# First four column tiles side by side, gate projections moved around the gated linear unit, one more step in the cross attention

## The chip, the cores and the metric

The kernel runs on one core of one Trainium2 chip. The metric is the device time of one execution in microseconds (us), less is better. TensorE does the matmuls, ScalarE (ACT in the profile) the activations and copies, VectorE (DVE) the elementwise arithmetic, GpSimd (POOL) a few helpers; SyncE (SP) issues the DMAs. Each engine takes its instructions in program order and waits on semaphores for the others.

## What is computed

One block of a transformer over 512 rows of 1024 columns, in single precision. The parts that the change touches:

```python
h = rmsnorm(x, g_mix_pre[l])
proj = h @ w_in[l]
a_out = pool_mixer(proj[..., OFF_POOL:OFF_ATT], pool_w[l], pool_scale[l])
b_out = dilated_attention(proj[..., OFF_ATT:OFF_SSM], rel_bias)
c_out = s5_mixer(proj[..., OFF_SSM:OFF_SGU], ...)      # ends in g * sigmoid(g @ w_glu + b_glu), g = gelu(y)
d_out = sgu_mixer(proj[..., OFF_SGU:OFF_GATE], ...)
gates = sigmoid(proj[..., OFF_GATE:].reshape(B, S, N_BRANCH, D_MODEL) + gate_b[l])
merged = sum over the four branches of gates[:, :, i] * (branches[i] @ w_up[l, i])
x = x + rmsnorm(merged @ w_out[l], g_mix_post[l])
x = x + rmsnorm(cross_attn(rmsnorm(x, g_x_pre[l]), rmsnorm(mem, g_mem[l]), w_cq[l], w_ckv[l], w_co[l]), g_x_post[l])
x = x + rmsnorm(square(relu(rmsnorm(x, g_ff_pre[l]) @ w_ff1[l])) @ w_ff2[l], g_ff_post[l])
```

The cross attention has four heads of 128 columns over 256 memory rows.

## The kernel before

Every large product is made of three matmuls: each operand is split into a high part (rounded to the matmul's format, a copy on ScalarE, L140) and a low part (the rest, a subtraction on VectorE, L144, L146, L208 or L310), and `mm3` (L237 to L239) adds high x high, low x high and high x low in one PSUM bank. There are eight banks, used in turn. Names with h and l at the end are the two parts: xh and xl of the input, wh and wl of a weight chunk, hh and hl of the normalized rows, bh and bl of a branch, cph and cpl of the transposed attention weights.

Weights come as chunks of 512 KB in one fixed order (`chunk_order`); `fetch` lets SP load the next one, `issue` splits it (the copy wh on ScalarE, L140, the subtraction wl on VectorE, L208), `chunk` hands the next one out and demands that the order fits. A chunk "P" in that order is split early and kept for later.

Everything that follows a matmul is a Python generator: each `yield` is one step. `later(g)` puts it in a list (`fore`, or `back` for long-running ones), and `tick()`, called between groups of 12 matmuls, lets every generator in the lists take one step and feeds the weight queue. So the place of an instruction in its engine's order is set by how many yields stand ahead of it, and by how many ticks the main program makes.

The start (L275 to L318, `first_pair`, `first`): the eight tiles xk of the input and the first two weight chunks arrive in pieces in turn; f0 and f1, the first two of six column tiles f, are done together, six matmuls for each k of eight, then f2 to f5 one after another, 24 matmuls each. `start()` squares the tiles xk on ScalarE (L646), adds them on VectorE (acc, L648 and L651), sums them over the partitions on TensorE (ssq, L329), and builds from them the row scale R (rb on TensorE, L341). It is a generator in `back`.

The gated linear unit (glu): y (L562) of the last of four groups goes through a gelu on ScalarE (gy); the loop `while len(gy) < 4: tick()` waits for the fourth; then the four gy are split (bh and bl), two ticks are made, and 48 matmuls glu follow. All the time a generator of the dilated attention runs in `back`: score matmuls L (L874, L876), exponentials Pm (L894), transposes PT (L900), outputs oA and oB (L923), spread by rA and rB (L997, L998). `gates` behind the glu makes, for each of four pairs of columns, two gate projections pj (24 matmuls each, then a Tanh gt on ScalarE, L803) and the products up.

The cross attention (`cross`, L1243 on): for each head and each half of the rows a generator does q split (cq), scores cL, row maxima, exponentials, their normalization (cP on VectorE, L1268), transposes (cT on TensorE, L1273), the split of these (cph, cpl), the product co with the values, and the split of that (bh and bl). Behind it the output projection nat takes pairs of chunks.

Of the kernel before, what the change touches and what calls it, by code (L numbers as in the profile page):

```python
# [52 lines left out]
def chunk_order():  # L53
# [5 lines left out]
    def gates(b):  # L59
        r = []  # L60
        for cp in range(4):
            r += [("L", "w_in", OFF_GATE + b * D + 128 * c) for c in (2 * cp, 2 * cp + 1)]
            r += [("U", "w_up", b, cp)]
        return r
# [9 lines left out]
    o += [("U", "w_glu", 0, cp) for cp in range(2)]  # L74
    o += gates(2)
# [10 lines left out]
    for c in range(4):  # L86
        o += [("L", "w_cq", 128 * c)]
        if c in (1, 3):
            o += [early.pop(0)]
# [15 lines left out]
def body(ctx: ExitStack, tc: tile.TileContext, xT, xn, memT, wch, vec, rows, cst, biasT, poolw, wsT, bst, cbd, out):  # L105
# [33 lines left out]
    def acopy(o, i, scale=1.0):  # L139
        act.activation(out=o, in_=i, func=AF.Copy, scale=scale)  # L140
# [18 lines left out]
    def later(g):  # L159
        fore.append(g)  # L160
# [22 lines left out]
    def fetch(parts=1):  # L183
        raw = wraw.tile([P, 1024], F32, name="wr", tag="wr")
        for i in range(parts):
            c = slice(1024 * i // parts, 1024 * (i + 1) // parts)
            sp.dma_start(out=raw[:, c], in_=wch[at[0]][:, c])
        raws.append(raw)
        at[0] += 1
# [89 lines left out]
    pair = [wraw.tile([P, 1024], F32, name="wr", tag="wr") for _ in range(2)]  # L279
    sp.dma_start(out=vt, in_=vec)  # L280
    for n, c in enumerate(PIECES):
        for j in range(2):
            sp.dma_start(out=pair[j][:, c], in_=wch[j][:, c])
            sp.dma_start(out=xk[2 * n + j], in_=xT[:, 2 * n + j])
    for k in (6, 7):
        sp.dma_start(out=xk[k], in_=xT[:, k])
    at[0] = 2
    fetch()
# [15 lines left out]
    pair_hl = [[whl.tile([P, 1024], F32R, name=n, tag="w") for n in ("wh", "wl")] for _ in range(2)]  # L304
    for n, c in enumerate(PIECES):
        for j in range(2):
            hi, lo = pair_hl[j]
            acopy(hi[:, c], pair[j][:, c])
            xsplit(2 * n + j)
            dve.tensor_sub(out=lo[:, c], in0=pair[j][:, c], in1=f32(hi[:, c]))  # L310
    for k in (6, 7):
        xsplit(k)
    at[1] = at[2] = 2
# [308 lines left out]
    def first_pair():  # L622

        bs = [bank(f"f{j}") for j in range(2)]
        for k in range(8):
            for j in range(2):
                hi, lo = (t[:, P * k:P * k + P] for t in pair_hl[j])
                mm3(bs[j], hi, lo, xh[k], xl[k], k == 0, k == 7)
        return bs
# [12 lines left out]
    def start():  # L642
        acc = [G("acc"), G("acc")]
        for k in range(8):
            sq = acc[k] if k < 2 else G("sq")
            act.activation(out=sq, in_=xk[k], func=AF.Square)  # L646
            if k > 1:
                dve.tensor_add(out=acc[k % 2], in0=acc[k % 2], in1=sq)  # L648
            if k == 3:
                issue()  # L650
        dve.tensor_add(out=acc[0], in0=acc[0], in1=acc[1])  # L651
        next(params)
        yield
        yield
# [47 lines left out]
    fb[0], fb[1] = first_pair()  # L702
    next(st_gen)
    sp.dma_start(out=pw, in_=poolw)
    back.append(st_gen)
    for i in range(2, 6):
        fb[i] = first(i)
# [88 lines left out]
    def gates(bi, br, last=None):  # L796
        bh, bl = br
        for cp in range(4):
            gt = {}

            def gate(c, b):
                gt[c] = G("gt")
                act.activation(out=gt[c], in_=b, func=AF.Tanh, scale=0.5, bias=gbh[:, 8 * bi + c:8 * bi + c + 1])  # L803
                yield
# [14 lines left out]
            for c in (2 * cp, 2 * cp + 1):  # L819
                later(gate(c, proj(("L", "w_in", OFF_GATE + bi * D + 128 * c), kth(hh), kth(hl))))  # L820
# [213 lines left out]

    while len(gy) < 4:
        tick()
# [23 lines left out]
    gates(2, ca)  # L1060
# [183 lines left out]
    def cross(c, s, b):  # L1244
# [33 lines left out]
        lo_of(pl, ph, tb)  # L1278
        yield
# [220 lines left out]
```

## Time and profile before

| what | value |
|---|---|
| median of 3 runs | 1148.78 us (1148.76 to 1148.9) |
| the profiled execution | 1150.06 us |
| its span | 1148.3 us |
| TensorE (PE) busy | 1133.5 us, 99% |
| VectorE (DVE) busy | 728.5 us, 63% |
| ScalarE (ACT) busy | 502.4 us, 44% |
| GpSimd (POOL) busy | 119.0 us, 10% |
| chain that ended last: PE, DVE, ACT | 93%, 3%, 1% |
| granted TensorE clock, mean | 0.995 |

The span runs from the first to the last instruction of the profiled execution; the time of an execution holds a little more (1.76 us here). A busy share is the share of the span in which an engine had work; TensorE's clock is given as a share of its full speed. The chain that ended last follows the work back from the last instruction to whatever released it.

### The profile page before, as it was taken

The page shows a single profiled execution, that of the slowest core. Times are in us where ns is not written, and L with a number is a line of the kernel's source. Part 1 is how long each engine was busy: PE and PEld are TensorE (multiplying, and loading weights), DVE is VectorE, ACT ScalarE, POOL GpSimd, SP SyncE. Part 2 cuts the span into 40 slices and gives each one's busy share as a digit, 9 for nine tenths or more (in the row PEclk, how much of TensorE's full clock was granted, in tenths as well). Part 3 has the DMA queues.
Part 4 walks back from the last instruction along what each step waited for, and adds up shares of the span by engine and source line. Part 5 has one row for each costly group of instructions (what it writes and reads, how often), then busy time and mean ns, then how long its engine had stood idle before and what let it go on. Part 6 is the DMA issues. An engine that isn't in the chain of part 4 may idle for free.

```text
span 1148.3 us, 15062 instructions
## 1 busy us (share of the span) xinstructions
PE 1133.5 (99%) x5720; PEld 943.6 (82%) x5720; DVE 728.5 (63%) x1185; ACT 502.4 (44%) x962; POOL 119.0 (10%) x200
## 2 busy tenths in 40 slices
PE   8999999999999999989999999999999999999997
PEld 6888887888987787767888888999988888888886
DVE  6798999997688677554355737777433334445343
ACT  7354444433446665564243436554332234344341
POOL 6960200000000000200100005003000000000001
PEclk9999999999999999989999999999999999999999
DMA  7523235323233222212243462710222332332221
GB/s 240 173 86 111 94 114 151 113 82 112 78 97 112 78 77 92 74 37 92 86 138 107 159 208 78 226 46 20 74 92 92 100 102 92 95 108 96 88 74 74
DMA packets 40025, 119.69 MB, mean 104 GB/s; under 512 B 5136, under 2 KB 7184, under 8 KB 39952
## 3 DMA queue, kind: packets, MB, share of 16 engines
q1 hardware_dynamic: 39952, 118.73, 32.2%
q8 instruction: 45, 0.74, 0.3%
q14 instruction: 28, 0.23, 0.1%
HBM read 113.47 MB, written 2.10 MB: 101 GB/s over the span
## 4 chain that ended last, share of the span: by engine, by line
PE 93%; DVE 3%; ACT 1%; issue 1%; SPq 1%; DMA 1%; POOL 0%; DVEq 0%; POOLq 0%; ACTq 0%
PE pj L237 16%; PE pj L239 15%; PE pj L238 15%; PE nat L237 10%; PE nat L238 10%; PE nat L239 10%; PE up L237 2%; PE up L238 2%; PE up L239 2%; PE PT L900 1%; PE f L239 1%; PE f L237 1%; PE f L238 1%; PE oA L923 1%; PE L L874 1%
## 5 line engine op out<-in xcount | busy, mean ns | idle before, releaser
L208 DVE TENSOR_TENSOR wl<-wr,wh 128x1024 fp32r<-128x1024 f32 x183 | 223.8, 1227 | 106.7 <-ACT wh L140 106.0
L140 ACT ACTIVATE wh<-wr 128x1024 fp32r<-128x1024 f32 (+1 forms) x189 | 194.4, 1032 | 65.3 <-PE pj L238 36.2
L237 PE MATMUL pj<-hh,wh 128*128 128x512 f32 x496 | 198.4, 400 | 0.0
L239 PE MATMUL pj<-hh,wl 128*128 128x512 f32 x496 | 193.7, 390 | 0.0
L238 PE MATMUL pj<-hl,wh 128*128 128x512 f32 x496 | 193.4, 390 | 0.0
L237 PEld LDWEIGHTS pj<-hh,wh 128*128 128x128 f32 x496 | 93.2, 188 | 21.7 <-issue 1.2
L239 PEld LDWEIGHTS pj<-hh,wl 128*128 128x128 f32 x496 | 93.1, 188 | 20.1
L238 PEld LDWEIGHTS pj<-hl,wh 128*128 128x128 f32 x496 | 93.3, 188 | 18.8 <-issue 0.5
L237 PE MATMUL nat<-wh,fh 128*128 128x512 f32 x256 | 99.6, 389 | 0.0
L238 PE MATMUL nat<-wl,fh 128*128 128x512 f32 x256 | 99.6, 389 | 0.0
L239 PE MATMUL nat<-wh,fl 128*128 128x512 f32 x256 | 99.6, 389 | 0.0
L144 DVE TENSOR_TENSOR fl<-f,fh 128x512 fp32r<-128x512 f32 x60 | 40.5, 691 | 73.3 <-PE nat L238 71.2
L237 PE MATMUL pj<-h3h,wh 128*128 128x512 f32 x216 | 84.0, 389 | 0.0
L238 PE MATMUL pj<-h3l,wh 128*128 128x512 f32 x216 | 84.0, 389 | 0.0
L239 PE MATMUL pj<-h3h,wl 128*128 128x512 f32 x216 | 84.0, 389 | 0.0
L1342 DVE TENSOR_TENSOR f<-fr,pj 128x512 f32<-128x512 f32 x32 | 22.0, 688 | 97.5 <-ACT fr L1340 97.5
L140 ACT ACTIVATE t<-tS,Ms 128x32 f32<-128x32 f32 (+1 forms) x64 | 25.3, 395 | 122.2 <-DVE tS L517 113.6
L140 ACT ACTIVATE fh<-f 128x512 fp32r<-128x512 f32 x60 | 37.0, 630 | 89.0 <-PE nat L238 85.7
L1340 ACT ACTIVATE fr<-pj 128x512 f32<-128x512 f32 x32 | 19.2, 599 | 116.8 <-PE pj L239 116.8
L237 PEld LDWEIGHTS nat<-wh,fh 128*128 128x128 f32 x256 | 48.1, 188 | 10.0
L238 PEld LDWEIGHTS nat<-wl,fh 128*128 128x128 f32 x256 | 48.1, 188 | 9.9
L239 PEld LDWEIGHTS nat<-wh,fl 128*128 128x128 f32 x256 | 48.1, 188 | 9.9
(327 smaller groups left out, 2312.5 us busy)
## 6 DMA issues: line engine op xcount, KB each, us to landing
wr<-in_wch SPq DMA_DIRECT2D x188, 512.0 KB, 3.5
row<-in_rows SPq DMA_DIRECT2D x13, 256.0 KB, 6.2
xk<-in_xT SPq DMA_DIRECT2D x8, 256.0 KB, 5.3
U<-uh SPq DMA_DIRECT2D x32, 64.0 KB, 2.0
bias<-in_biasT SPq DMA_DIRECT2D x8, 256.0 KB, 3.9
x<-in_xn SPq DMA_DIRECT2D x8, 256.0 KB, 5.2
out_dram<-x SPq DMA_DIRECT2D x8, 256.0 KB, 2.0
braw<-in_bst SPq DMA_DIRECT2D x16, 96.0 KB, 3.6
```

The source lines that it names most:

```text
L140: act.activation(out=o, in_=i, func=AF.Copy, scale=scale)
L144: dve.tensor_sub(out=lo, in0=src, in1=f32(hi))
L208: dve.tensor_sub(out=lo[:, c], in0=raw[:, c], in1=f32(hi[:, c]))
L237: pe.matmul(out=o, lhsT=lh, rhs=rh, start=start, stop=False)
L238: pe.matmul(out=o, lhsT=lh, rhs=rl, start=False, stop=False)
L239: pe.matmul(out=o, lhsT=ll, rhs=rh, start=False, stop=stop)
L874: pe.matmul(out=L[:, lo:lo + 256], lhsT=q[0][a][e, s], rhs=k[0][b][e, ks], start=n == 0, stop=n == 2)
L900: pe.transpose(out=b[:, s:s + 128], in_=Pm[:, s:s + 128], identity=ident)
L923: pe.matmul(out=o_[O][e, s], lhsT=V[v][:, cs], rhs=o[h][:, 128 * n:128 * n + 128], start=n == 0 or n == 2 or (n == 1 and i == 0), stop=n % ...
L1340: act.activation(out=r, in_=b, func=AF.Relu)
L1342: dve.tensor_mul(out=t, in0=r, in1=b)
```

## The change

Four things, by place in the program:

- The start. Four weight chunks (in place of two) arrive in pieces, in turn with the tiles xk, and are split in pieces; `first_four` does f0 to f3 side by side, 12 matmuls for each k; only f4 and f5 go one after another. The generator `start()` runs up to its first yield ahead of these matmuls, and gets its next two steps from within them, behind k = 5 and behind k = 6; it has two yields less ahead of ssq.
- The glu. The two gate projections of the first column pair of the third branch (`gate_pair(2, 0)`) stand ahead of the loop that waits for the gelu, those of the second pair behind the glu matmuls, and `gates` takes them as given. The chunk order follows.
- One early chunk "P" stands behind the third w_cq chunk, not the fourth.
- `cross` has one more yield between the split cph, cpl and the product co.

```diff
@@ -71,8 +71,8 @@
     for hp in range(NPAIR):
         for g in range(3):
             o += [("L", "w_in", OFF_Q + 512 * g + 128 * hp), ("L", "w_in", OFF_K + 512 * g + 128 * hp)]
-    o += [("U", "w_glu", 0, cp) for cp in range(2)]
-    o += gates(2)
+    ahead = gates(2)
+    o += ahead[:2] + [("U", "w_glu", 0, cp) for cp in range(2)] + ahead[3:5] + [ahead[2]] + ahead[5:]
     o += gates(1)
     early = [("P", "w_ff1", 128 * c) for c in range(NPRE)]
     for h in range(2):
@@ -85,7 +85,7 @@
         o += [("R", "w_ckv", k, 512)]
     for c in range(4):
         o += [("L", "w_cq", 128 * c)]
-        if c in (1, 3):
+        if c in (1, 2):
             o += [early.pop(0)]
     o += [("R", "w_co", k, 512 * h) for k in range(2) for h in range(2)]
     o += [("L", "w_ff1", 128 * c) for c in range(NPRE, 32)]
@@ -276,16 +276,19 @@
     xl = [G("xl", F32R) for k in range(8)]
 
     PIECES = (slice(0, 256), slice(256, 512), slice(512, 1024))
-    pair = [wraw.tile([P, 1024], F32, name="wr", tag="wr") for _ in range(2)]
+    four = [[t[:, c] for c in PIECES] for t in (wraw.tile([P, 1024], F32, name="wr", tag="wr") for _ in range(3))]
+    g0, g1 = G("wr0"), G("wr1")
+    four.append([g0[:, 0:256], g0[:, 256:512], g1])
     sp.dma_start(out=vt, in_=vec)
     for n, c in enumerate(PIECES):
-        for j in range(2):
-            sp.dma_start(out=pair[j][:, c], in_=wch[j][:, c])
-            sp.dma_start(out=xk[2 * n + j], in_=xT[:, 2 * n + j])
-    for k in (6, 7):
-        sp.dma_start(out=xk[k], in_=xT[:, k])
-    at[0] = 2
-    fetch()
+        ks = (2 * n, 2 * n + 1) if n < 2 else (4, 5, 6, 7)
+        for j in range(4):
+            if j % 2 and j // 2 < len(ks):
+                sp.dma_start(out=xk[ks[j // 2]], in_=xT[:, ks[j // 2]])
+            sp.dma_start(out=four[j][n], in_=wch[j][:, c])
+        for k in ks[2:]:
+            sp.dma_start(out=xk[k], in_=xT[:, k])
+    at[0] = 4
     sp.dma_start(out=ct, in_=cst)
     dve.memset(ones, 1.0)
     dve.memset(mhalf, -0.5)
@@ -301,16 +304,18 @@
         acopy(xh[k], xk[k], gx(k))
         lo_of(xl[k], xh[k], xk[k], gx(k))
 
-    pair_hl = [[whl.tile([P, 1024], F32R, name=n, tag="w") for n in ("wh", "wl")] for _ in range(2)]
+    four_hl = [[whl.tile([P, 1024], F32R, name=n, tag="w") for n in ("wh", "wl")] for _ in range(4)]
     for n, c in enumerate(PIECES):
-        for j in range(2):
-            hi, lo = pair_hl[j]
-            acopy(hi[:, c], pair[j][:, c])
-            xsplit(2 * n + j)
-            dve.tensor_sub(out=lo[:, c], in0=pair[j][:, c], in1=f32(hi[:, c]))
-    for k in (6, 7):
-        xsplit(k)
-    at[1] = at[2] = 2
+        ks = (2 * n, 2 * n + 1) if n < 2 else (4, 5, 6, 7)
+        for j in range(4):
+            hi, lo = four_hl[j]
+            acopy(hi[:, c], four[j][n])
+            if j % 2 == 0 and j // 2 < len(ks):
+                xsplit(ks[j // 2])
+            dve.tensor_sub(out=lo[:, c], in0=four[j][n], in1=f32(hi[:, c]))
+        for k in ks[2:]:
+            xsplit(k)
+    at[1] = at[2] = 4
 
     def rstd(o, ss, n, scale):
 
@@ -619,13 +624,15 @@
         yield from split(pa[0][g], pa[1][g], o, vt[:, V_POOLS + g:V_POOLS + g + 1])
 
 
-    def first_pair():
-
-        bs = [bank(f"f{j}") for j in range(2)]
+    def first_four(beside):
+
+        bs = [bank(f"f{j}") for j in range(4)]
         for k in range(8):
-            for j in range(2):
-                hi, lo = (t[:, P * k:P * k + P] for t in pair_hl[j])
+            for j in range(4):
+                hi, lo = (t[:, P * k:P * k + P] for t in four_hl[j])
                 mm3(bs[j], hi, lo, xh[k], xl[k], k == 0, k == 7)
+            if k in (5, 6):
+                next(beside)
         return bs
 
     def first(i):
@@ -647,11 +654,10 @@
             if k > 1:
                 dve.tensor_add(out=acc[k % 2], in0=acc[k % 2], in1=sq)
             if k == 3:
+                fetch()
                 issue()
         dve.tensor_add(out=acc[0], in0=acc[0], in1=acc[1])
         next(params)
-        yield
-        yield
         yield
         sb = bank("ssq")
         sums(sb, acc[0], 4)
@@ -699,11 +705,11 @@
     next(params)
     st_gen = start()
     fb = [None] * 6
-    fb[0], fb[1] = first_pair()
     next(st_gen)
+    fb[:4] = first_four(st_gen)
     sp.dma_start(out=pw, in_=poolw)
     back.append(st_gen)
-    for i in range(2, 6):
+    for i in range(4, 6):
         fb[i] = first(i)
     dve.tensor_scalar(out=gbh, in0=vt[:, V_GATEB:V_GATEB + 32], scalar1=0.5, scalar2=None, op0=MUL)
     dve.tensor_scalar(out=bgh, in0=vt[:, V_BGLU:V_BGLU + 4], scalar1=0.5, scalar2=None, op0=MUL)
@@ -793,15 +799,22 @@
 
     merged = {}
 
-    def gates(bi, br, last=None):
+    def gate_pair(bi, cp):
+        gt = {}
+
+        def gate(c, b):
+            gt[c] = G("gt")
+            act.activation(out=gt[c], in_=b, func=AF.Tanh, scale=0.5, bias=gbh[:, 8 * bi + c:8 * bi + c + 1])
+            yield
+
+        for c in (2 * cp, 2 * cp + 1):
+            later(gate(c, proj(("L", "w_in", OFF_GATE + bi * D + 128 * c), kth(hh), kth(hl))))
+        return gt
+
+    def gates(bi, br, last=None, ahead=None):
         bh, bl = br
         for cp in range(4):
-            gt = {}
-
-            def gate(c, b):
-                gt[c] = G("gt")
-                act.activation(out=gt[c], in_=b, func=AF.Tanh, scale=0.5, bias=gbh[:, 8 * bi + c:8 * bi + c + 1])
-                yield
+            gt = ahead[cp] if ahead and cp < 2 else gate_pair(bi, cp)
 
             def up(c, b, gt):
                 if c not in merged:
@@ -816,8 +829,6 @@
                 if last:
                     yield from last(c)
 
-            for c in (2 * cp, 2 * cp + 1):
-                later(gate(c, proj(("L", "w_in", OFF_GATE + bi * D + 128 * c), kth(hh), kth(hl))))
             wh, wl = chunk("U", "w_up", bi, cp)
             for cc in range(2):
                 b = bank("up")
@@ -1032,6 +1043,7 @@
         back.append(run())
 
 
+    ahead = [gate_pair(2, 0)]
     while len(gy) < 4:
         tick()
     ga = branch()
@@ -1057,7 +1069,8 @@
                 mm3(b, wh[:, cc, k], wl[:, cc, k], ga[0][k], ga[1][k], k == 0, k == 3)
             tick()
             later(glu(2 * cp + cc, b))
-    gates(2, ca)
+    ahead.append(gate_pair(2, 1))
+    gates(2, ca, ahead=ahead)
     while back:
         tick()
     WB[0] = NBIG // 2
@@ -1276,6 +1289,7 @@
         ph, pl = G("cph", F32R), G("cpl", F32R)
         acopy(ph, tb)
         lo_of(pl, ph, tb)
+        yield
         yield
         o = bank("co")
         for m in range(2):
```

Where it moves instructions, in three places. `[waits ...]` names the engines, or DMA queues, on which an instruction waits.

TensorE in the start, around ssq. Before, in f3, f_351 (the fourth column tile, behind f0, f1 and f2):

```order
L239 MATMUL f_351<-xh,wl 128x512
L329 MATMUL ssq<-ones,acc 128x1 x4
L237 MATMUL f_351<-xh,wh 128x512
L238 MATMUL f_351<-xl,wh 128x512
L239 MATMUL f_351<-xh,wl 128x512
```

Now (f_284 to f_287 are the first four column tiles, f_287 with k = 5 ahead of ssq, f_284 with k = 6 behind it):

```order
L237 MATMUL f_287<-xh,wh 128x512
L238 MATMUL f_287<-xl,wh 128x512
L239 MATMUL f_287<-xh,wl 128x512
L334 MATMUL ssq<-ones,acc 128x1 [waits DVE_49]
L334 MATMUL ssq<-ones,acc 128x1 x3
L237 MATMUL f_284<-xh,wh 128x512 [waits Activation_49]
L238 MATMUL f_284<-xl,wh 128x512
```

ssq has moved from behind 84 f matmuls (48 of the pair, 24 of f2, 12 of f3) to behind 72 and waits for VectorE there; 24 f matmuls, in place of 12, stand between it and the first of f4.

ScalarE ahead of the glu. Before (gy is the gelu, oAs and oBs copy attention outputs, bh splits the four gelu results, Pm are the exponentials):

```order
L140 ACTIVATE wr<-x_4582 16x512 [waits PE_49]
L571 ACT_TABLE_LOAD
L571 ACTIVATE gy_4613<-ys 128x512 [waits DVE_49]
L140 ACTIVATE oAs<-oA 128x512 [waits PE_49]
L140 ACTIVATE oBs<-oB 128x4x128 [waits DMAHW4_49,PE_49]
L140 ACTIVATE bh_4626<-gy_1913 128x512 [waits DMAHW5_49]
L140 ACTIVATE bh_4627<-gy_2654 128x512 [waits Activation_49]
L140 ACTIVATE bh_4628<-gy_3465 128x512
L140 ACTIVATE bh_4629<-gy_4613 128x512 [waits Activation_49]
L894 ACT_TABLE_LOAD
L894 ACTIVATE Pm,stA<-Pm,stA 128x128 [waits DVE_49]
```

Now:

```order
L807 ACTIVATE gt<-pj,gbh 128x512 [waits PE_49]
L140 ACTIVATE wr<-x_4626 16x512 [waits PE_49]
L576 ACT_TABLE_LOAD
L576 ACTIVATE gy_4690<-ys 128x512 [waits DVE_49]
L140 ACTIVATE oAs<-oA 128x512 [waits DMAHW0_49,PE_49]
L140 ACTIVATE oBs<-oB 128x4x128 [waits PE_49,Activation_49]
L807 ACTIVATE gt<-pj,gbh 128x512 [waits PE_49]
L140 ACTIVATE bh_4703<-gy_1926 128x512
L140 ACTIVATE bh_4704<-gy_2667 128x512 [waits Activation_49]
L140 ACTIVATE bh_4705<-gy_3478 128x512 [waits Activation_49]
L140 ACTIVATE bh_4706<-gy_4690 128x512 [waits Activation_49]
L905 ACT_TABLE_LOAD [waits DMAHW1_49]
```

Two Tanh gt have moved in, one ahead of the copy wr and one between oBs and the four bh; each waits for its gate projection on TensorE. The rest keeps its order. On TensorE the first projection stands in two halves of 12 matmuls ahead of y, the second in two halves of 12 between x (L989 before) and rA.

TensorE in the cross attention, where the last scores are done. Before, two steps (cT of the fifth and sixth, co of the fourth of eight):

```order
L1273 MATMUL cT<-ct,cP 128x128 [waits DVE_49] x2
L1273 MATMUL cT<-ct,cP 128x128 x2
L237 MATMUL co<-cph,vh_6583 128x256 [waits Activation_49]
L238 MATMUL co<-cpl,vh_6583 128x256 [waits DVE_49]
L239 MATMUL co<-cph,vl_6584 128x256
L237 MATMUL co<-cph,vh_6626 128x256
L238 MATMUL co<-cpl,vh_6626 128x256
L239 MATMUL co<-cph,vl_6627 128x256
L1273 MATMUL cT<-ct,cP 128x128 [waits DVE_49] x2
L1273 MATMUL cT<-ct,cP 128x128 x2
L237 MATMUL nat<-wh,bh_6586 128x512
L238 MATMUL nat<-wl,bh_6586 128x512
```

Now, from the same cT (the fifth) on, with the co of the third:

```order
L1286 MATMUL cT<-ct,cP 128x128 [waits DVE_49] x2
L1286 MATMUL cT<-ct,cP 128x128 x2
L237 MATMUL co<-cph,vh_6596 128x256 [waits Activation_49]
L238 MATMUL co<-cpl,vh_6596 128x256
L239 MATMUL co<-cph,vl_6597 128x256
L237 MATMUL co<-cph,vh_6639 128x256
L238 MATMUL co<-cpl,vh_6639 128x256
L239 MATMUL co<-cph,vl_6640 128x256
L1286 MATMUL cT<-ct,cP 128x128 [waits DVE_49,Activation_49]
L1286 MATMUL cT<-ct,cP 128x128 [waits DVE_49]
L1286 MATMUL cT<-ct,cP 128x128 x2
```

Each co stands one step later, and no longer waits for cpl (the wait for VectorE in its second matmul is gone); behind this cT comes another co, and the first nat stands one step later too.

## Rows read from the trace of the kernel before

**Rows 1.** TensorE's waits, the longest; engine, line, waited for: us, times, longest.
```profile
PE PT L900 <- ACT Pm L894: 4.2, 1, 4.2
PE f L239 <- DVE wl L310: 1.4, 2, 1.0
...
PE co L238 <- DVE cpl L144: 1.0, 1, 1.0
```

**Rows 2.** Timeline of TensorE at the glu: start, length, engine, line, instruction, [idle before].
```profile
490.98 0.50 PE L997 MATMUL rA<-wr,selr 16*128 16x512 f32 x1
...
496.90 1.18 PE L900 MATMUL PT<-ct,Pm 128*128 128x128 f32 x3 [4.18 <-ACT Pm L894]
...
502.56 0.40 PE L239 MATMUL glu<-bh,wl 128*128 128x512 f32 x1
```

**Rows 3.** Timeline of ScalarE at the same place.
```profile
492.84 2.20 ACT L140 ACTIVATE bh<-gy 128x512 fp32r<-128x512 f32 x4
495.05 1.28 ACT L894 ACT_TABLE_LOAD   x1
496.35 0.40 ACT L894 ACTIVATE Pm<-Pm,stA 128x128 f32<-128x128 f32 x1
...
503.00 0.69 ACT L1046 ACTIVATE gl<-glu,bgh 128x512 f32<-128x512 f32 x1 [2.48 <-PE glu L239]
```

**Rows 4.** Windows at the glu: engines' busy us, granted clock, DMA share, GB/s.
```profile
495.50:495.75 0.25, 0.00 (x0) 0.00 (x0) 0.25 (x1) 0.25 (x1) 0.00 (x0) 0.94 0.00 0
495.75:496.00 0.25, 0.00 (x0) 0.00 (x0) 0.25 (x2) 0.25 (x1) 0.00 (x0) 0.50 0.00 0
...
502.50:502.75 0.25, 0.25 (x2) 0.00 (x0) 0.00 (x0) 0.00 (x0) 0.00 (x0) 0.91 1.12 442
```

**Rows 5.** Timeline of TensorE in the start.
```profile
5.61 0.49 PE L237 MATMUL f<-xh,wh 128*128 128x512 f32 x1
...
23.05 0.39 PE L237 MATMUL f<-xh,wh 128*128 128x512 f32 x1
...
28.49 0.95 PE L329 MATMUL ssq<-ones,acc 128*128 128x1 f32 x8
...
32.16 0.39 PE L237 MATMUL f<-xh,wh 128*128 128x512 f32 x1
```

**Rows 6.** Timeline of VectorE in the start.
```profile
10.06 0.75 DVE L146 SCALAR_TENSOR_TENSOR xl<-xk,vt,xh 128x512 fp32r<-128x512 f32 x1 [1.43 <-ACT xh L140]
10.73 0.52 DVE L310 TENSOR_TENSOR wl<-wr,wh 128x256 fp32r<-128x256 f32 x1
...
13.19 0.98 DVE L310 TENSOR_TENSOR wl<-wr,wh 128x512 fp32r<-128x512 f32 x1
...
22.83 0.69 DVE L651 TENSOR_TENSOR acc<-acc 128x512 f32<-128x512 f32 x1
```

**Rows 7.** Window in the start, columns as in rows 4.
```profile
10.00:15.00 5.00, 4.79 (x19) 3.13 (x18) 4.91 (x8) 4.94 (x10) 4.50 (x7) 1.00 1.01 380
```

**Rows 8.** Timeline of VectorE in the cross attention.
```profile
755.39 0.69 DVE L144 TENSOR_TENSOR cpl<-cT,cph 128x512 fp32r<-128x512 f32 x1 [1.55 <-ACT cph L140]
...
757.85 0.41 DVE L144 TENSOR_TENSOR bl<-co,bh 128x256 fp32r<-128x256 f32 x1
...
763.86 0.62 DVE L1268 TENSOR_SCALAR cP<-cP,cst 128x256 f32<-128x256 f32 x2
```

**Rows 9.** Timeline of TensorE in the cross attention.
```profile
760.02 0.36 PE L237 MATMUL co<-cph,vh 128*128 128x256 f32 x1
...
762.06 0.60 PE L1273 MATMUL cT<-ct,cP 128*128 128x128 f32 x4
762.42 0.48 PE L237 MATMUL nat<-wh,bh 128*128 128x512 f32 x1
...
764.61 0.60 PE L1273 MATMUL cT<-ct,cP 128*128 128x128 f32 x4
...
771.79 0.40 PE L237 MATMUL nat<-wh,bh 128*128 128x512 f32 x1
```

## Prediction

> **What bounds the kernel now.** I read the busy table first: TensorE works 1133.5 of 1148.3 us, and nothing else comes near. So the time is TensorE's own work plus the few microseconds in which it stands. The change adds or removes no matmul, and this leaves three things that can move the end: TensorE's waits, its clock, and new waits that another order brings in. The list of its waits is short [rows 1]: one of 4.2 us (PT behind an exponential on ScalarE), two that make 1.4 us in the first matmuls (f behind wl of VectorE), one of 1.0 us in the cross attention (co behind cpl). The change has one edit for each. So I read each place in the timeline of TensorE and of the engine it waits for, and then ask of the new order what is late there next. The profiled execution took 1150.06 us, 1.76 over its span and 1.28 over the median of 1148.78; the sum below is made of differences against that execution, and I carry them to the median unchanged.
>
> **The gated linear unit: what it costs now.** From the last score matmuls to PT TensorE stands 4.18 us [rows 2]. ScalarE meanwhile works without a gap [rows 3]: the four splits bh (492.84 to 495.05, 2.21 us), a table load (1.30 to the next start), the first exponential (0.55 to PT at 496.90). There is a second price. The granted clock falls from 1.00 to 0.50 at about 495.7, that is 3.0 us after TensorE went idle at 492.72, and is back at 502.5 [rows 4]. In between PT and eleven glu matmuls go at half rate: all but the last 0.1 of the 5.66 us from 496.90 to 502.56 [rows 2]. At full rate they would take half of it, so the fall costs about 2.75 us, and the place 6.9 in all.
>
> **What the edit does there.** Two gate projections of 24 matmuls each (5.45 us) come forward, in halves of 12, between y, the oA/oB, L and rA/rB matmuls. They are moved, not added; their weights move with them in the chunk order, and the second pair lies behind the glu with the cover that the first had. On ScalarE two Tanh are moved too. The first (gt) ends before the gelu and is out of the way. The second stands in ScalarE's order between oBs and the four bh, and waits for the end T of the second projection. Queued behind it are the bh, the table load, the exponentials, and with them PT. From T on ScalarE needs 0.04 + 0.6 (the Tanh of a 128x512 bank, by gl [rows 3]: it starts 0.04 after its last matmul's end; 0.69 long, some 0.1 of it beside the next) + 2.21 + 1.30 + 0.55 = 4.7 us to PT. TensorE has rA, rB and L left, 490.98 to 492.72 [rows 2], 1.74 us, which overlap the projection's tail by some 0.15. The wait is 4.7 - 1.6 = **3.1 us**: 1.1 less, not 4.2 less. The projections fill time before the chain, but the chain from the bh to PT starts only behind them.
> Whether the clock holds is the larger part. It fell 3.0 us into the idle time, and the new idle time is 3.1. I take it that it holds, for the fall would come at the very end of it and the stretch before is now dense (projections in place of short matmuls): -1.1 - 2.75 = **-3.8**. If it falls, the stretch at half rate is 6.8 us by [rows 4] with next to no idle time in it, so 3.4 us lost: 3.1 + 3.4 against 6.9, **-0.4**. The ends are -6.9 (no wait at all) and 0.
>
> [...]
>
> **The start.** Now f0 and f1 go together, from 5.61 on, and f2 to f5 follow; ssq stands at 28.49 and the 97th f matmul starts at 32.16 [rows 5]. One f matmul takes 0.227 at full pace (24 of them between 23.05 and 28.49), ssq with its restart 32.16 - 28.49 - 12 x 0.227 = 0.9. So the 96 and ssq would take 22.7 without waits, and 3.85 us are lost. With four columns a step of k holds 12 matmuls (2.7 us) in place of 6, and the wait for wl late in the start goes. The first step still waits: f2 and f3 need wl pieces that stand behind the second xl in VectorE's order. I keep 2.0 to 2.4 us of loss in the first two steps, so the 72 matmuls of six steps end near 5.61 + 72 x 0.227 + 2.2 = 24.2.
> But ssq now stands behind those 72 matmuls, ahead of the last 24, and needs the sum of squares, which is VectorE's last piece of a row without gaps. Before, this row runs from xl at 10.06 to 22.83 + 0.61, 13.4 us [rows 6]. The change puts four more pieces into it, two of 128x256 and two of 128x512: 2 x (0.52 + 0.98) less 0.08 overlap each (0.75 from 10.06 against a next start at 10.73) = 2.7. It also starts later, for two more pieces of 128 KB arrive ahead of the third xk: 0.26 MB at 380 GB/s [rows 7], 0.7 us. So acc is ready at 10.75 + 13.4 + 2.7 = 26.85, and TensorE, at 24.2, **waits 2.6 us for it**. Then 0.9 for ssq and 24 x 0.227 = 5.45: the 97th matmul starts at 33.1, **+0.9** over 32.16. Ends: the row does not get longer because the added pieces fill gaps (acc 2 us earlier, ssq waits 0.6): -1.1; the pieces arrive another microsecond later: +1.9. What follows, rb and R, leans on ssq, which is earlier than before: no cost.
>
> **The cross attention.** A head's step gains a yield between cph/cpl and co, so co comes a step later in the order. Before, co waits 1.0 us for cpl, just behind cT and in front of the next cT. With the step, cpl is long there; the price is what TensorE then reaches too early. VectorE works from 755.39 on without a gap until past 763.86, and each cT needs cP from that same row: the seventh (cT6) needs cP at 763.86 + 0.62. The move of co puts one bl (0.41 long, 0.33 of it without the overlap of 0.08 as above) behind it, so cP is ready at 764.15 [rows 8]. TensorE's order up to cT5 holds the same pieces as up to 760.02 before, and then cT5 and co: it could be at cT6 at 761.1 to 762. It waits, here and at cT5, until 764.15, whichever way these waits are split. From there two times cT, nat, co (762.06 to 764.61, 2.55) and two times nat, co (2.19) follow: 764.15 + 9.48 = 773.6, where the next nat started at 771.79 [rows 9]. **+1.8**: the last steps hold a co that earlier stood in VectorE's shadow. Ends: -1.0 (only the old wait goes) and +2.2.
> The early w_ff1 chunk that moves from behind the fourth w_cq column to behind the third costs nothing: its copy and subtraction are done in a stretch that has no TensorE wait in [rows 1], and it is one chunk at an adjacent place. If that cover fails it delays one cq by a subtraction of some 1.2 us.
>
> **Sum.** -3.8 + 0.9 + 1.8 = -1.1: 1149.0 against 1150.06, on the median **1147.7**.
>
> **Rivals.**
> The clock falls all the same. Slower side, one mechanism: the idle time before PT, 3.1 us, is as long as that after which it fell before. Then the glu brings -0.4, and -0.4 + 0.9 + 1.8 = +2.3 gives 1151.1 (1149.3 to 1152). It decides from about 3.0 us of idle time on; against it speaks that the idle time is a quarter shorter. [...]
> The covers work as the edits read. If VectorE's row is not the limit in the start (-1.1) or in the cross attention (-1.0), either alone takes 2 to 2.8 off: 1144.9 to 1145.7; both, 1142.9. For it: in the start VectorE idled before its row began [rows 6]. Against it: the row has no gaps afterwards, and the 5.0 us by which acc was ready ahead of ssq before (23.44 against 28.49) go to 12 fewer matmuls ahead of ssq (2.7), an earlier end of the others (1.5) and the longer, later row (3.4).
> The glu edit does not do what it says. If something else is in ScalarE's way (a wh copy of 1.05 in front of the bh), the wait is 4.2 again and the clock falls: +0 + 0.9 + 1.8, 1151.5.
>
> **Chances.** The sum with the clock kept 0.46 (1146.2 to 1149.2 on its own); the clock falls 0.27; a cover works as read 0.16; no effect at the glu 0.07; rest 0.04. The range 1144.8 to 1151.6 leaves out the case of both covers and the upper part of the two slow ones. A difference of 0.2%, 2.3 us, is about what a measurement can tell from none. Faster than 1146.5: most of the cover cases and the lower edge of the first, 0.23. Slower than 1151.1: half of the falling clock, most of no effect, 0.21. Between: 0.56.
>
> **What would show it.** TensorE's list of waits should have PT near 3.1 us, ssq behind acc near 2.6, cT behind cP twice with 2.5 to 3.0 together, and no co. The granted clock around the glu should stay at 1.00, and the glu matmuls follow each other at 0.23, not at twice that. The 97th f matmul should start near 33.1, the nat behind the last co some 1.8 later than the same place would otherwise lie. If ssq does not wait, my length of VectorE's row is wrong; if PT waits under 2 us, ScalarE's order behind the second Tanh is not what binds; if the clock is at 0.50 in the glu, the first rival holds.

## The result, and the profile after

The changed kernel takes 1156.02 us, the median of 5 runs from 1152.86 to 1157.69, against 1148.9 (1148.76 to 1149.81): 0.6% slower, ratio 1.0056, interval 1.004 to 1.0073. The forecast was 1147.7 with a range up to 1151.6. The single times now lie 4.8 us apart, those of before 1.1. The profiled execution took 1155.07 us with a span of 1153.3; TensorE is busy 1135.1 us of it, so it stands 18.2 us in place of 14.8, and the busy time of the same work is 1.6 us longer. The lower clock explains some 0.4 of these 1.6: matmuls went at half rate for 6.4 us (27.15 to 30.57 and 512.26 to 515.26, below) in place of 5.6 before, and half of the difference is lost. Where the rest comes from was not traced.

TensorE's list of waits after (us, times, longest), to be laid beside [rows 1]:

```profile
PE PT L911 <- ACT Pm L905: 3.0, 1, 3.0
PE ssq L334 <- DVE acc L659: 1.8, 1, 1.8
PE pj L237 <- DVE svt L789: 1.5, 1, 1.5
PE f L239 <- DVE wl L315: 1.2, 1, 1.2
...
PE cT L1286 <- DVE cP L1281: 1.0, 1, 1.0
PE cT L1286 <- ACT bh L140: 1.0, 1, 1.0
PE po L622 <- DVE pp L618: 0.7, 1, 0.7
```

PT waits 3.0 in place of 4.2 and co not at all, as forecast. Against that stand ssq 1.8, cT twice 1.0, both forecast, and two that were not: pj behind svt 1.5 and po behind pp 0.7, both behind VectorE and both far behind the start (116 and 94.5 us).

Then the clock. Windows of the changed kernel, columns as in [rows 4], the granted clock third from the end:

```profile
27.00:27.50 0.50, 0.50 (x4) 0.50 (x5) 0.08 (x1) 0.00 (x0) 0.00 (x0) 0.65 0.00 0
30.00:30.50 0.50, 0.50 (x3) 0.40 (x2) 0.50 (x1) 0.00 (x0) 0.50 (x1) 0.50 0.00 0
30.50:31.00 0.50, 0.50 (x4) 0.41 (x3) 0.41 (x1) 0.00 (x0) 0.50 (x2) 0.94 0.00 0
...
511.75:512.00 0.25, 0.00 (x0) 0.00 (x0) 0.25 (x1) 0.25 (x1) 0.00 (x0) 0.69 0.00 0
515.25:515.50 0.25, 0.25 (x2) 0.20 (x2) 0.25 (x1) 0.25 (x3) 0.00 (x0) 0.99 0.00 0
```

Leaving out the last ten microseconds, where it goes down in both kernels (0.50 in the last 2.3 us before, 0.52 in the last 3.3 after), it falls to 0.50 twice, not once: from about 27.15 to 30.55, at ssq, and from about 511.85 to 515.25, at the glu. The timeline of TensorE at ssq (compare [rows 5]):

```profile
24.09 0.39 PE L239 MATMUL f<-xh,wl 128*128 128x512 f32 x1
26.28 1.10 PE L334 MATMUL ssq<-ones,acc 128*128 128x1 f32 x8 [1.80 <-DVE acc L659]
27.25 0.78 PE L237 MATMUL f<-xh,wh 128*128 128x512 f32 x1
...
28.67 0.63 PE L237 MATMUL f<-xh,wh 128*128 128x512 f32 x1
...
34.37 0.39 PE L237 MATMUL f<-xh,wh 128*128 128x512 f32 x1
```

TensorE is idle from 24.48 to 26.28, does the narrow ssq matmuls, and 0.9 us after it resumed the clock is down; the f matmuls follow each other at 0.43 in place of 0.23. The 97th f matmul starts at 34.37, 2.2 us later than before (32.16). The nat behind the last co starts at 776.69, against 771.79 [rows 9]: by then 4.9 us are lost, all that the span has grown by (5.0). Two places between divide this: at the pj that waits for svt TensorE is 5.1 us late (116.06 against 110.92), at the rb of the next norm, behind the merged branches, 3.3 (627.03 against 623.72). So in this execution the start lost 5.1, the glu won 1.8 and the cross attention lost 1.6.

### The profile page after: what moved, and what is told of

Its sections match the earlier page's. It is cut to its first block, busy times and chain, and to the rows that moved or that the text cites. A ratio compares the mean times of both kernels' runs of the same rounds, so it can differ in the third digit from the quotient of the medians.

```text
span 1153.3 us, 15079 instructions
## 1 busy us (share of the span) xinstructions
PE 1135.1 (98%) x5720; PEld 945.0 (82%) x5720; DVE 726.0 (63%) x1189; ACT 503.4 (44%) x966; POOL 113.5 (10%) x200
## 4 chain that ended last, share of the span: by engine, by line
PE 86%; DVE 3%; issue 1%; ACT 1%; SPq 1%; DMA 0%; POOL 0%; DVEq 0%; POOLq 0%; ACTq 0%
PE pj L237 15%; PE pj L239 15%; PE pj L238 15%; PE nat L237 9%; PE nat L239 9%; PE nat L238 9%; PE up L237 2%; PE up L238 2%; PE up L239 2%; PE PT L911 1%; PE oA L934 1%; PE L L885 1%; PE y L567 1%; PE oB L934 1%; PE ht L1196 1%
## 5 line engine op out<-in xcount | busy, mean ns | idle before, releaser
L140 ACT ACTIVATE wh<-wr 128x1024 fp32r<-128x1024 f32 (+2 forms) x193 | 195.0, 1015 | 69.0 <-PE pj L238 39.4
```

## The experiments

**One part at a time.** Three kernels take one part of the change each and leave the rest as before.

start_only, the four column tiles (one line of its edit; the pieces of the DMAs and the yields of `start()` go with it):

```diff
-    fb[0], fb[1] = first_pair()
+    fb[:4] = first_four(st_gen)
```

> The kernel before with the four column tiles in the start alone (glu and cross attention as before). Theory A, the start carries the loss: ssq waits 1.8 us behind acc and the clock falls there (1.7 us), then po waits 0.7 and pj behind svt 1.5, since VectorE is 5 us late. By the landmarks of the changed kernel TensorE is 5.1 us behind at 116 us, so +5 on the median of 1148.9: 1153 to 1155, and the single times spread by some 2 us since the clock falls in some executions only. Theory B, the loss comes from how the parts act together: the start alone stays within 1 us of before.

Measured: 1153.95 us (1151.99 to 1155.65), ratio 1.004, 1.0028 to 1.0053: **+5.1** on its before of 1148.86. The profiled execution is the shortest of the five; there ssq waits only 1.3 us and the clock holds in the start (1.00 in each window from 24 to 36 us). It shows the rest of the loss by itself:

```profile
PE PT L906 <- ACT Pm L900: 4.2, 1, 4.2
PE pj L237 <- DVE svt L789: 1.4, 1, 1.4
PE ssq L334 <- DVE acc L659: 1.3, 1, 1.3
...
PE po L622 <- DVE pp L618: 0.7, 1, 0.7
```

Theory A holds: the start carries the loss, and the waits behind svt and pp come with it even though TensorE is not late at the 97th f matmul here (31.95 against 32.16).

glu_only, the gate pairs (parts of its edit; the chunk order goes with it):

```diff
+    ahead = [gate_pair(2, 0)]
     while len(gy) < 4:
         tick()
...
-    gates(2, ca)
+    ahead.append(gate_pair(2, 1))
+    gates(2, ca, ahead=ahead)
```

> The kernel before with the two gate pairs around the glu alone. Theory A: PT waits 3.0 us in place of 4.2, the second Tanh stands ahead of the four bh. If the clock falls there too, as in the changed kernel, 1.7 us are lost in place of 2.75: -2.0, 1146.9; if it holds, -3.8, 1145.1. Theory B, the moved projections cost elsewhere (weight stream): 1148.5 or more.

Measured: 1147.92 us (1147.31 to 1148.8, 11 runs), ratio 0.9991, 0.9983 to 1.0: **-0.9**. In its profile PT waits 3.0, and the clock falls there for 6.8 us (504.76 to 511.59):

```profile
504.50:505.00 0.50, 0.00 (x0) 0.00 (x0) 0.50 (x2) 0.50 (x1) 0.00 (x0) 0.76 0.00 0
511.50:512.00 0.50, 0.50 (x3) 0.14 (x2) 0.00 (x0) 0.00 (x0) 0.00 (x0) 0.91 0.97 401
```

```profile
506.05 1.18 PE L905 MATMUL PT<-ct,Pm 128*128 128x128 f32 x3 [3.00 <-ACT Pm L899]
```

The time is between the two theories' numbers. The wait shrinks by 1.2 as theory A says; the half rate lies over 5.5 us of PT and glu matmuls (506.05 to 511.59), about as much as the 5.66 before, so it costs what it cost and only the shorter wait is won.

yield_only, the step in the cross attention without the moved chunk:

```diff
         lo_of(pl, ph, tb)
         yield
+        yield
         o = bank("co")
```

> The kernel before with the one yield in the cross attention alone (the early chunk stays behind the fourth w_cq column). Theory A, VectorE sets the last cP and a co is left over at the end: +1.8 to +2.3, 1150.7 to 1151.2, with waits of cT in place of co. Theory B, the wait of 1.0 goes and nothing takes its place: 1147.9.

Measured: 1150.89 us (1150.4 to 1152.08, 11 runs), ratio 1.0019, 1.001 to 1.0027: **+2.0**, theory A. The timelines of TensorE and then of VectorE (cP) in this kernel:

```profile
760.70 0.72 PE L1273 MATMUL cT<-ct,cP 128*128 128x128 f32 x4 [0.99 <-ACT bh L140]
...
763.14 0.72 PE L1273 MATMUL cT<-ct,cP 128*128 128x128 f32 x4 [1.02 <-DVE cP L1268]
```

```profile
760.20 0.62 DVE L1268 TENSOR_SCALAR cP<-cP,cst 128x256 f32<-128x256 f32 x2
...
762.64 0.62 DVE L1268 TENSOR_SCALAR cP<-cP,cst 128x256 f32<-128x256 f32 x2
```

Both cT start 0.5 us behind the start of their cP, and VectorE has no gap between the two. The trace names bh for the first of them; that it is cP there too is argued from these rows only.

**The second Tanh.** glu_late lets the Tanh of the first pair come one step later, and nothing else differs from glu_only:

```diff
         def gate(c, b):
+            if late:
+                yield
             gt[c] = G("gt")
```

> As glu_only (1147.92), but the Tanh of the first pair's projections come one step later, so that the second stands behind the four bh and the first exponentials on ScalarE. Theory A, the second Tanh holds the bh, the table load and the exponentials back: PT waits at most about 1 us in place of 3.0, the clock holds there, and 2.0 plus 1.7 to 2.75 come off: 1143.2 to 1144.3, single times within 1 us but for other falls of the clock. Theory B, PT is bound by the scores L behind rA and rB and by VectorE: a wait of 2.5 or more, 1147 or more.

Measured: **1143.72 us** (1143.5 to 1143.99), ratio 0.9955, 0.9942 to 0.9967: 5.1 under its before, 4.2 under glu_only. The wait of PT is gone, and the clock holds through the glu, whose matmuls follow each other at 0.23. ScalarE first, then TensorE:

```profile
497.92 1.09 ACT L140 ACTIVATE oBs<-oB 128x512 f32<-128x512 f32 x1
498.79 2.19 ACT L140 ACTIVATE bh<-gy 128x512 fp32r<-128x512 f32 x4
501.00 1.28 ACT L901 ACT_TABLE_LOAD   x1
502.30 0.40 ACT L901 ACTIVATE Pm<-Pm,stA 128x128 f32<-128x128 f32 x1
...
503.19 0.66 ACT L803 ACTIVATE gt<-pj,gbh 128x512 f32<-128x512 f32 x1
```

```profile
503.38 0.55 PE L907 MATMUL PT<-ct,Pm 128*128 128x128 f32 x3
503.69 0.47 PE L237 MATMUL glu<-bh,wh 128*128 128x512 f32 x1
504.75 0.50 PE L238 MATMUL glu<-bl,wh 128*128 128x512 f32 x1 [0.59 <-DVE bl L144]
```

The bh, the table load and the first exponential now run beside the second projection and the short matmuls behind it, and what is left is 0.6 us for bl. The edit moves both Tanh of the pair; it is the second that stood ahead of the bh. So the second Tanh held them back, and with them 3 us of wait and the clock. The single times lie within 0.5 us, those of before within 2.0 in the same series (1147.88 to 1149.83 over 11 runs). That the clock at the glu is what spreads the times of before is argued from this, and the clock of each execution bears it out: of 21 executions of before, measured beside start_only, the seven with a mean granted clock of 0.998 took 1147.89 to 1148.86 us, the six with 0.995 1149.41 to 1150.08.

**The start, ssq.** start_ssq sets ssq behind all 96 matmuls:

```diff
-            if k in (5, 6):
-                next(beside)
+        next(beside)
+        next(beside)
         return bs
```

> As start_only (1153.95, single times 1152.0 to 1155.7), but ssq stands behind all 96 matmuls of the four columns, not behind 72. Theory A: the wait of ssq for acc (1.3 to 1.8 us) goes, and with it the fall of the clock that some executions have there; the waits of po and svt stay. So 1.3 to 1.8 plus about 1 on the mean off the median, 1151 to 1151.7, and the single times lie closer together (within 2 us). Theory B: the spread and the loss do not come from ssq: 1153.5 or more, same spread.

Measured: 1152.03 us (1151.54 to 1153.07, 7 runs): 1.9 under start_only, and the spread falls from 3.7 to 1.5. That is theory A for ssq, though the time stays above the 1151 to 1151.7 expected. In the profiled execution TensorE is 1.8 us ahead of before at the 97th matmul, and has given it all back at po, for which it waits 1.7 in place of 0.7:

```profile
30.34 0.49 PE L237 MATMUL f<-xh,wh 128*128 128x512 f32 x1
...
92.09 1.10 PE L622 MATMUL po<-pp,pw 128*128 128x512 f32 x2 [1.68 <-DVE pp L618]
```

This po starts at 91.47 before and at 92.16 in start_only, so the lead of 1.8 us does not get past it; the clock falls behind that wait (0.50 from about 93.7 to 97.2 us).

The same again in glu_late, whose profile (mean granted clock 0.999) shows no fall of the clock ahead of the last microseconds, so that what the start does to it stands alone. late_start is glu_late with the start of the change, late_ssq has also the edit above:

> As glu_late, with the start of the change. No other place loses the clock on this ground, so what the times spread is the start's alone. Theory A: the start costs 2.7 us without and 4.4 to 6 us with a falling clock at ssq or later: 1146.4 to 1149.8, median about 1148.7, single times spread by 2 us or more. Theory B, the start's loss in start_only was made larger by the glu behind it: 1146 or less.

> As late_start, with ssq behind all 96 matmuls; it differs from all_mended (1144.26) only in u and hk standing behind the next wl on VectorE. Theory A1, that wl holds VectorE back and with it po and svt: 1146.4 to 1147.2, 2 to 3 us over all_mended, the wait in front of po near 1.7. Theory A2, its place does not matter: within 0.7 of all_mended.

Measured: late_start 1150.3 us (1147.92 to 1151.66, 11 runs), **+6.6** over glu_late; late_ssq 1147.05 (1146.65 to 1147.37, 11 runs), +3.3. These two were measured in another series than glu_late and all_mended, with 1149.04 for before in place of 1148.8, so differences between the series are sure to some 0.3 us only. late_start is more than expected. Its profiled execution is the longest of the 11; ssq waits 2.9 us there, and the clock stays at half for 6.8 us:

```profile
26.91 1.86 PE L334 MATMUL ssq<-ones,acc 128*128 128x1 f32 x8 [2.92 <-DVE acc L659]
28.64 0.77 PE L237 MATMUL f<-xh,wh 128*128 128x512 f32 x1
```

```profile
26.00:28.00 2.00, 1.09 (x6) 1.09 (x6) 0.82 (x2) 1.45 (x4) 0.00 (x0) 0.70 0.29 117
28.00:30.00 2.00, 2.00 (x7) 1.77 (x8) 0.16 (x1) 0.00 (x0) 0.88 (x1) 0.50 0.00 0
32.00:34.00 2.00, 2.00 (x6) 1.53 (x6) 0.31 (x1) 0.00 (x0) 1.92 (x8) 0.60 0.25 51
34.00:36.00 2.00, 2.00 (x10) 1.65 (x9) 0.00 (x0) 0.00 (x0) 1.84 (x8) 1.00 0.55 219
```

So the wait at ssq with its clock costs 3.25 us on the median (1150.3 - 1147.05), although po then waits 1.1 us longer without it (1.7 against 0.6), and it makes the spread (3.7 against 0.7). The six executions of late_start with a mean clock of 0.996 or less took 1150.3 to 1151.66, the five with more 1147.92 to 1150.03. Of late_ssq 3.3 us are left, with waits of 1.7 at po and 1.5 at svt.

**The start, VectorE behind R.** Before, u starts as soon as R is copied; ScalarE's and VectorE's rows of the kernel before:

```profile
35.97 0.60 ACT L140 ACTIVATE R<-rb 128x512 f32<-128x512 f32 x1 [3.98 <-PE rb L341]
...
36.60 0.69 DVE L479 TENSOR_TENSOR u<-f,R 128x512 f32<-128x512 f32 x1 [2.43 <-ACT R L140]
```

In start_only the copy R is no later, but u waits for another subtraction, whose wh stands behind R on ScalarE; ScalarE, then VectorE:

```profile
35.77 0.60 ACT L140 ACTIVATE R<-rb 128x512 f32<-128x512 f32 x1 [10.04 <-PE rb L346]
36.26 1.05 ACT L140 ACTIVATE wh<-wr 128x1024 fp32r<-128x1024 f32 x1
```

```profile
37.34 1.23 DVE L208 TENSOR_TENSOR wl<-wr,wh 128x1024 fp32r<-128x1024 f32 x1 [7.30 <-ACT wh L140]
38.48 0.68 DVE L484 TENSOR_TENSOR u<-f,R 128x512 f32<-128x512 f32 x1
```

VectorE stands 7.3 us, and then does in the critical moment what it had done early before: with four columns at once, six chunks are split by the time that R comes, in place of eight. In the changed kernel R itself is late too. Its rb stands 12 f matmuls behind the 97th in TensorE's order (34.88 before, 37.09 now), so R follows TensorE and not ssq, and u starts 4.6 us later than before (41.20 against 36.60), 2.2 of it through R and 2.4 through wl; ScalarE, then VectorE:

```profile
38.18 0.60 ACT L140 ACTIVATE R<-rb 128x512 f32<-128x512 f32 x1 [11.61 <-PE rb L346]
```

```profile
39.75 1.53 DVE L208 TENSOR_TENSOR wl<-wr,wh 128x1024 fp32r<-128x1024 f32 x1 [8.84 <-ACT wh L140]
41.20 0.68 DVE L484 TENSOR_TENSOR u<-f,R 128x512 f32<-128x512 f32 x1
```

start_R puts u and hk ahead:

```diff
         acopy(R, r)
-        yield
         hk = {}
```

> As start_only, without the yield behind the copy R, so that u and hk stand ahead of the next wl in VectorE's order. Theory A1, VectorE's 5 us delay in the start is half due to that wl, whose wh stands behind R on ScalarE (u at 41.2 in place of about 38.8): the waits of po and of pj behind svt, 2.2 us and what follows, shrink to under 0.7, and the time is 1.5 to 2.5 us below start_only; ssq and the clock stay as there. Theory A2, the delay is the total of VectorE's work: the time is that of start_only within 0.7.

Measured: 1155.27 us (1153.91 to 1156.82), 1.3 over start_only. A1 holds in the trace up to 128 us: u starts at 36.32, the waits of po and svt are gone. But with one yield less the whole state-space part runs a step earlier, and at 132 us a new one stands, with a fall of the clock behind it (the pj follow each other at 0.43 there):

```profile
132.00 0.76 PE L237 MATMUL pj<-hh,wh 128*128 128x512 f32 x1 [2.71 <-ACT t L140]
132.56 0.63 PE L238 MATMUL pj<-hl,wh 128*128 128x512 f32 x1
```

start_R2 gives the yield back behind the second hk, so that the steps behind it stay:

```diff
         acopy(R, r)
-        yield
         hk = {}
...
         l_(0)
+        yield
         back.append(ssm())
```

> As start_only (1153.95), with u and hk of the first two tiles one step earlier, ahead of the next wl on VectorE, but with the yield given back behind them, so that the state-space part keeps its steps. In start_R the waits of po and of svt went (TensorE 0.4 ahead of before up to 128 us in place of 2.7 behind), and then a wait of 2.7 us for t came up at 131 us with a falling clock. Theory A1, that wait comes from the shifted steps of the state-space part: here it is absent, the waits of po and svt stay under 1 us together, 1151.5 to 1152.5. Theory A2, VectorE's work in this stretch is late anyhow and only the place of the wait moves: 1153 or more.

Measured: 1153.39 us (1151.48 to 1155.72), 0.6 under start_only with a spread of 4 us. The new wait is absent, svt's is gone, po's is 0.6; in the profiled execution, with a mean granted clock of 0.995, the clock falls at ssq, behind a wait of 1.8. By the time alone this decides nothing.

all_mended decides it: the start with both edits (ssq behind the 96, u and hk ahead as in start_R2), and glu_late:

> The changed start with ssq behind the 96 matmuls and u, hk ahead of wl, and the two gate pairs with the later Tanh; the cross attention as before. By theory A the parts add: the start costs about +1 over before, the glu brings -4.6 to -5.7, so 1144 to 1145.5. If the start's parts act against each other (another place where VectorE is late), 1146 or more.

Measured: 1144.26 us (1143.72 to 1144.97), ratio 0.996, 0.9947 to 0.9972. It differs from late_ssq (1147.05) by nothing but the place of u and hk: **2.8 us** (2.5 if each is taken against before in its own series), A1. The pj behind svt, which started at 110.92 before, in late_ssq and then in all_mended:

```profile
113.00 0.47 PE L237 MATMUL pj<-hh,wh 128*128 128x512 f32 x1 [1.49 <-DVE svt L789]
```

```profile
110.87 0.48 PE L237 MATMUL pj<-hh,wh 128*128 128x512 f32 x1
```

Its start still costs 0.5 over glu_late: TensorE is 1.7 ahead of before at 30.5 us and level with it at 110.9. It waits 1.0 for po on the way; the rest of the lead was not traced.

**The moved chunk, and the yield again.** late_P is glu_late with the early chunk behind the third w_cq column, late_PY has the yield too:

```diff
-        if c in (1, 3):
+        if c in (1, 2):
```

> As glu_late (1143.72, single times 1143.5 to 1144.0, a ground without a falling clock), with the early w_ff1 chunk behind the third w_cq column as in the change. Theory A, the move costs nothing: 1143.4 to 1144.1. Theory B, the parts measured alone (+5.1, -0.9, +2.0) lack about 1 us to the whole change (+7.1), and this move is it: 1144.5 to 1145.

> As late_P, with the yield in the cross attention. Theory A, VectorE sets the last two cT and a co is left over: +1.8 to +2.3 over late_P, 1145.5 to 1146.2, cT waiting 1.0 us twice for cP. Theory B, the yield costs less on a ground without a falling clock: +1 or less, 1144.8.

Measured: late_P 1143.55 us (1143.5 to 1143.85), the same as glu_late: the move costs nothing. late_PY 1145.05 (1144.53 to 1146.9): +1.5 for the yield, between the two theories, with the two waits of 1.0 for cT. Its single times spread by 2.4 us at a mean clock of 0.998 to 0.999 in all five, so the clock is not the only thing that spreads times.

The parts measured alone make +5.1 - 0.9 + 2.0 = +6.2, the whole +7.1. The difference is smaller than the spread of single times (4.8), and what it is stays open.

## Why the prediction was wrong

**What it read rightly.** What is late next, at each of three places: PT waits 3.0 (3.1 forecast) because the second Tanh holds the bh back, which glu_late shows; ssq waits for acc, 1.8 (2.6 forecast; 1.3 to 2.9 in other executions); cT waits twice for cP, 2.0 together (2.5 to 3.0), and the step costs 1.5 to 2.0 (+1.8 forecast). The chunk costs nothing.

Of these, the time of acc was in part luck. The forecast had it at 26.85, from a row of VectorE that starts 0.7 us later and has no gaps; it came at 26.22, from a row that starts as early as before (10.03) and stands 1.6 us for the fifth tile xk:

```profile
14.65 0.75 DVE L146 SCALAR_TENSOR_TENSOR xl<-xk,vt,xh 128x512 fp32r<-128x512 f32 x1 [1.61 <-ACT xh L140]
```

With the same start, start_only has 0.4 us there and ssq waits 1.3; late_start has two gaps, 1.0 and 1.2, and ssq waits 2.9. ScalarE's copies ahead of these gaps wait for DMAs (1.7 us for the fifth xk in the changed kernel, 1.6 for a chunk in late_start), so the wait at ssq differs from one execution to the next with the arrival of tiles and chunks.

**"What follows, rb and R, leans on ssq, which is earlier than before: no cost" is the step that failed.** It put at nothing what is the larger part of the start's loss in the profiled execution: 2.2 us are lost up to the 97th f, and 2.9 more from there to the pj behind svt. R does not lean on ssq but on the place of rb in TensorE's order, so that it comes 2.2 us later though ssq comes 2.2 earlier. And the step asked when R is ready, not what stands in VectorE's order ahead of the work on R. The order does show it: wl, wl, then u. The second wl had been done early before; now its wh stands behind R on ScalarE. That is 2.1 us on u in start_only (38.48 against the end of R at 36.37), and 2.8 us of time (late_ssq against all_mended), paid at 94 and 116 us.

**The clock at ssq has no price in it.** The forecast worked out a wait of 2.6 us at ssq and priced it as 2.6 us. It asked for the clock only at the glu. In the profiled execution the wait was 1.8, and the half rate behind it, 3.4 us long, took another 1.7: the 97th f came 2.2 late, not 0.9. On the median the wait with its clock costs 3.25 us (late_start against late_ssq). With the step above this makes the term that was given as +0.9 and measured +5.1 (+6.6 beside the later Tanh).

**The clock at the glu: the rival came true.** The forecast took it that the clock holds, "for the fall would come at the very end" of an idle time of 3.1 us. It fell 2.6 us into 3.0 in the changed kernel and 1.7 us into the same wait in glu_only. Nor do "about 3.0 us of idle time" decide, as the rival has it. The wait of 4.18 us of the kernel before, with the same matmuls ahead of it, stands in start_only too; before, the clock fell 3.0 us into it and stayed at half for 6.8 us, here it fell 4.1 us into it, at 499.61, and stayed for 3.4:

```profile
499.50:500.00 0.50, 0.27 (x1) 0.18 (x1) 0.50 (x3) 0.50 (x4) 0.00 (x0) 0.61 0.00 0
```

```profile
499.73 1.18 PE L906 MATMUL PT<-ct,Pm 128*128 128x128 f32 x3 [4.18 <-ACT Pm L900]
```

So one and the same idle stretch had two outcomes; what decides between them no run shows.

The first rival gave -0.4 for this part; measured alone it is -0.9, for the -3.8 of the sum.

**The sum of the misses.** The median is 8.3 us over the forecast. Rounded, 4.2 of it is the start (+5.1 for +0.9), 2.9 the glu (-0.9 for -3.8), 0.2 the cross attention, and 0.9 is what the parts measured alone do not show. The whole rival gave 1151.1, and what lacks to 1156 is mainly the start.

**The bounds.** The end of +1.9 for the start came from a later arrival of pieces. Neither the clock at ssq nor the queue behind R was in any bound, so the range stopped 4.4 us short of the median.

## What to carry to other kernels

A new wait on TensorE is priced as its length and, as a second case with a chance of its own, the half clock behind it (at ssq 3.4 us of it in the changed kernel, 6.8 in late_start); a wait whose length hangs on the arrival of data spreads the times as well (late_start by 3.7 us, late_ssq without that wait by 0.7). When a change consumes inputs in parallel, ask which splits or loads were done early in the old order and now stand in the in-order queue ahead of the urgent work (here one wl, 2.1 us on u in start_only). Before work is moved in front of a wait, look at what it puts into the queue of the engine that is waited for: here the gain of the move (5.1 us against 0.9) hung on the Tanh of one pair, one step later.

## What the runs showed of the hardware

One and the same wait can lose the clock at different points of it. The 4.2 us for PT, with the same matmuls ahead, stand in six profiled executions: the clock fell 1.4 us (start_R), 2.1 (start_R2), 2.3 (yield_only), 3.0 (before) and 4.1 us (start_only) after TensorE went idle, and in start_ssq 0.15 us after it had resumed. It stayed at half for 6.8 us in the first four and for 3.4 in the last two. At ssq both were seen too: 3.4 in the changed kernel, 6.8 in late_start.

Shorter waits can lose it too, or not. At ssq it fell 0.9 us after the end of a wait of 1.8; waits of 1.3 and 1.4 there (start_only, start_R) left it at full. A wait of 1.7 at po was followed by a fall in start_ssq and by none in late_ssq.

With no such wait (glu_late) single times agreed within 0.5 us.
